# Five ring buffers for gathered rows and weights become seven of two kinds, and ten more u tiles move ahead of the last loop

## The chip, the cores and the metric

The kernel runs on one core of a Trainium2 chip. The time is device microseconds of one launch, the median of the runs of a kernel. It is one step of a streaming encoder layer (RWKV-7 mixing, sparse attention, PEER experts) for 256 prompt tokens and 8 x 16 sample tokens, in float32 throughout. Matmuls that must be exact split each operand into a rounded upper half and a remainder ("hi" and "lo", type fp32r) and add three products.

## The reference, cut to what matters

The change lies in the last part of the layer, the PEER experts. Each token picks 16 of 16,384 experts for each of 8 heads (128 experts in all), takes its dot product with their rows of `peer_u`, and adds their rows of `peer_v` with the weights that follow.

```python
def block(hb):
    ...
    e = jnp.take_along_axis(cidx, j, axis=-1)
    g = jax.nn.softmax(sc, axis=-1)
    act = jax.nn.gelu(jnp.einsum('nhkd,nd->nhk', peer_u[e], hb).astype(jnp.float32))
    return jnp.einsum('nhk,nhkd->nd', (g * act).astype(hb.dtype), peer_v[e])
...
x = x + g2 * _peer(h2, lp['w_pq'], lp['peer_keys'], lp['peer_u'], lp['peer_v'])
```

## The kernel before, in words

The first thousand microseconds (projections, RWKV, attention, mixing, choice of experts) are not touched. The rest computes the experts in two ways at once.

**The sample tokens, sparsely** (`peer_sparse`). For each of the 128 picks of a token one "row" is made: GpSimd issues an indirect DMA (line 1593) that gathers, for the 128 tokens on the 128 partitions, the u and the v row of the chosen expert side by side, 2,048 floats per partition, 1.05 MB in all. VectorE then forms the dot product with u (line 1600), ScalarE takes the gelu and the weight (1601, 1602), and VectorE adds the weighted v row to `acc` (1606). The buffer is `raw`, from `ring()`, with EB = 3 buffers: the gather of a row waits for the `acc` instruction of the row three before it. In the last loop each gather waits also for the matmuls of the v tile five before (`pace`, line 1742).

**The prompt tokens, densely.** All 16,384 experts are run for all 256 tokens in 128 tiles of 128 experts. `dense_u(j)` loads a u tile (512 KB), multiplies it with the tokens and puts the gelu into G[j]; `dense_v(j)` loads a v tile (512 KB) and accumulates G[j] times it into four PSUM banks (`bx`, `cp`, and two `dx`). G holds NW = 76 tiles of 256 floats per partition. The other 52 go to smaller tiles: 24 of them ("OFF", NB = 24) are written to DRAM from `gO` and loaded back into `gB` when needed, the others stay in 8 `gA` buffers.

The order in the program is: u tiles 0 to 41 with plain float32 matmuls; u tiles 42 to 75 with hi/lo halves; then 64 steps that make the matrix of weights and multiply G by it (`weights`), between which `ahead` adds u tiles from the list AHEAD (24 OFF and 7 more, 31 in all, at UR = 0.5 per step); then the loop over the 128 v tiles, which also makes the 21 u tiles left. Into all this `pull` weaves the rows, at a rate per step given by SR: 0.5 per u tile from tile 30 on, 0.5 per weight step, 0.62 per v tile, which makes 6, 17, 32 and 73 rows. A v tile is split into halves (lines 233 and 237, `wh` on ScalarE and `wl` on VectorE) except every third one up to the 108th, which is multiplied in plain float32.

**Buffers for tiles.** u and v tiles share a ring of four buffers `w` of 1,024 floats (`self.slots`). In the last loop the tiles of G are used up in rising order, and the kernel adds their space to the ring: after v tiles 3, 7, ... 31 four tiles of G at a time, eight buffers in all, so that the ring grows from four to twelve. A load into such a buffer shows in the trace as `G<-in_pv` or `G<-in_puT`.

**What sets the order.** A scheduler places the instructions of each engine by its own model of time, so that an engine's order isn't that of the program; on the chip each engine then runs its list strictly in order, and so does SP, which issues the direct DMAs. After the 123rd v tile come the last parts of the rows' result (`residual(0, ...)`), after the loop `finish_v` closes the four banks one by one and `residual` (lines 1576 to 1578) multiplies, adds and stores them.

Of the kernel before, what the change touches and what calls it, by code (L numbers as in the profile page):

```python
# [177 lines left out]
ORDER = "GGIggggR1R23DMMMGRMRDMRGMGMRMDGMMRRMGDMMMGGGMGGM"  # L178


N1, NW, NA, NB = 42, 76, 8, 24
SCORES, TURNS = 18, (21, 39)
SR, UR = (0.5, 0.5, 0.62), 0.5
S0, PH = 30, 4
OFF = [j for j in range(NW, 128) if (j - NW + 1) * NB // (128 - NW) > (j - NW) * NB // (128 - NW)]
AHEAD = sorted(OFF + [j for j in range(NW, 128) if j not in OFF][:NA - 1])
LAST, EARLY, SLOTS = 126, 108, 8
WB, EB = (4, 4, 3), 3
UENG, VENG, GENG, VN = 'v', 'v', 'g', 3
SENG = 'gv'  # L190
# [7 lines left out]
class K:  # L198
    def __init__(self, ctx, tc, I, O):
        self.ctx, self.tc, self.nc, self.I, self.O = ctx, tc, tc.nc, I, O  # L200
        self.uid = 0
        self.const = self.open(ctx, "const")
        self.stream = self.open(ctx, "stream")
        self.dram = self.open(ctx, "dram", space=bass.MemoryType.DRAM)
        self.nlo = 0
        self.slots = deque([None] * WB[0])
        self.lo_pattern = "v"

    def open(self, ctx, name, **kw):
# [1259 lines left out]

    def ring(self):  # L1470

        r = self.t([128, 2048], tag="raw", bufs=EB, pool=self.peer)
        return r[:, :1024], r[:, 1024:]

    def expert(self, src):

        s = self.slots.popleft()
        self.slots.append(s)
        if s is None:
            w = self.t([128, 1024], tag="w", bufs=WB[0], pool=self.stream)  # L1480
        else:
            w = self.G[:, 4 * s:4 * s + 4].rearrange("p a b -> p (a b)")
        self.nc.sync.dma_start(w, src)
        return w

# [124 lines left out]
    def run(self):  # L1610
# [79 lines left out]
        def pull(rate):  # L1690
            sn[0] += rate
            while sn[0] >= 1:
                sn[0] -= 1
                next(sparse, None)
# [46 lines left out]
        for n, j in enumerate(order):  # L1741
            self.pace = self.vdone[n - 5] if n > 4 else None
            pull(SR[2])
            while todo and sum(u not in OFF for u in gs) < NA - 1:
                u = todo.pop(0)
                gs[u] = self.dense_u(u)
            last.append(self.dense_v(j, gs.pop(j) if j >= NW else self.G[:, j], out, n))
            if j < 4 * SLOTS and j % 4 == 3:
                self.slots.append(j // 4)
            if n == 122:  # L1750
                for _ in sparse:
                    pass
                (a, b), (y, _) = self.ring(), self.ring()
                self.residual(0, [self.acc[:, c * 512:c * 512 + 512] for c in range(2)], self.gate2(0, a), self.x1_rows(0, b), y)
                (a, b), (c, y1), (y2, _) = (self.ring() for _ in range(3))
                g, x1, y = self.gate2(1, a), [self.x1_rows(1, b), self.x1_rows(2, c)], (y1, y2)
# [28 lines left out]
```

## Time and profile before

| | before |
|---|---|
| median of 3 runs | 1776.36 us (1776.22 to 1776.38) |
| the profiled execution | 1775.95 us |
| its span, first to last instruction | 1773.9 us |
| TensorE busy | 1664.8 us, 94% |
| VectorE busy | 1354.5 us, 76% |
| ScalarE busy | 750.9 us, 42% |
| GpSimd busy | 549.8 us, 31% |
| DMA | 437.22 MB, mean 246 GB/s |
| mean granted TensorE clock | 0.971 |

2.05 us of the profiled execution lie outside its span. PE is TensorE, PEld its loads of weights, DVE VectorE, ACT ScalarE, POOL GpSimd, SP the engine that issues direct DMAs. A line of the trace names the output, then the inputs; "x58" counts instructions; the bracket at its end is the idle time of the engine before it and what ended it. Neither TensorE's busy share nor a mean of one matmul tells its speed, since matmuls overlap: their starts do, 0.227 us apart for 512 columns in fp32r and about 0.118 us for 256. The page's 40 slices are 44.3 us each.

### The profile page before, as it was taken

The page shows a single profiled execution, that of the slowest core. Times are in us where ns is not written, and L with a number is a line of the kernel's source. Part 1 is how long each engine was busy: PE and PEld are TensorE (multiplying, and loading weights), DVE is VectorE, ACT ScalarE, POOL GpSimd, SP SyncE. Part 2 cuts the span into 40 slices and gives each one's busy share as a digit, 9 for nine tenths or more (in the row PEclk, how much of TensorE's full clock was granted, in tenths as well). Part 3 has the DMA queues.
Part 4 walks back from the last instruction along what each step waited for, and adds up shares of the span by engine and source line. Part 5 has one row for each costly group of instructions (what it writes and reads, how often), then busy time and mean ns, then how long its engine had stood idle before and what let it go on. Part 6 is the DMA issues. An engine that isn't in the chain of part 4 may idle for free. (4 is left out here: it accounts for less than half of the span.)

```text
span 1773.9 us, 33227 instructions
## 1 busy us (share of the span) xinstructions
PE 1664.8 (94%) x12376; PEld 1412.1 (80%) x12376; DVE 1354.5 (76%) x2905; ACT 750.9 (42%) x1666; POOL 549.8 (31%) x621
## 2 busy tenths in 40 slices
PE   6999999999999988999999989999999999999970
PEld 4898788878878866998887889999876777777750
DVE  4449788878768845566999998999766676777896
ACT  4533433333333233444222365678733343434531
POOL 2434243333332310034123223431233123223332
PEclk8999999999999999999999999999999999999995
DMA  8543752463364276655598989986499989999957
GB/s 296 164 141 99 214 173 72 157 202 110 102 220 143 79 260 209 211 177 187 188 374 322 347 326 390 381 296 203 168 377 404 357 331 360 338 343 338 333 211 258
DMA packets 173049, 437.22 MB, mean 246 GB/s; under 512 B 46036, under 2 KB 86612, under 8 KB 156504
## 3 DMA queue, kind: packets, MB, share of 16 engines
q1 hardware_dynamic: 154456, 300.89, 50.2%
q0 software_dynamic: 18432, 134.23, 20.0%
q8 instruction: 97, 1.59, 0.4%
q14 instruction: 64, 0.52, 0.1%
HBM read 403.75 MB, written 31.30 MB: 245 GB/s over the span
## 5 line engine op out<-in xcount | busy, mean ns | idle before, releaser
L1593 POOL DMA_INDIRECT raw<-in_puv,pe x128 | 177.3, 1385 | 501.9 <-DVE acc L1606 319.7
L237 DVE TENSOR_TENSOR wl<-w,wh 128x1024 fp32r<-128x1024 f32 x208 | 261.1, 1260 | 91.8 <-ACT wh L233 35.3
L233 ACT ACTIVATE wh<-w 128x1024 fp32r<-128x1024 f32 x216 | 226.9, 1053 | 152.0 <-PE mm L229 71.0
L229 PE MATMUL fx<-h2h,wh 128*128 128x256 f32 x688 | 196.5, 286 | 0.2 <-ACT G L1509 0.2
L229 PE MATMUL fx<-h2h,wl 128*128 128x256 f32 x688 | 193.9, 283 | 2.1 <-DVE wl L237 2.1
L229 PE MATMUL fx<-h2l,wh 128*128 128x256 f32 x688 | 193.6, 282 | 0.0
L1606 DVE SCALAR_TENSOR_TENSOR acc<-raw,dots,acc 128x1024 f32<-128x1024 f32 x127 | 163.5, 1287 | 21.4 <-ACT dots L1602 20.6
L1600 DVE SCALAR_TENSOR_TENSOR raw<-raw,sh 128x1024 f32<-128x1024 f32 x128 | 159.8, 1249 | 15.2 <-DMA raw<-in_puv,pe 15.1
L229 PEld LDWEIGHTS fx<-h2h,wl 128*128 128x128 f32 x688 | 130.0, 189 | 3.7 <-DVE wl L237 3.1
L229 PEld LDWEIGHTS fx<-h2h,wh 128*128 128x128 f32 x688 | 129.9, 189 | 2.5 <-issue 1.2
L229 PEld LDWEIGHTS fx<-h2l,wh 128*128 128x128 f32 x688 | 129.7, 189 | 2.2 <-issue 1.7
L229 PE MATMUL mm<-LTh,wh 128*128 128x384 f32 (+2 forms) x352 | 123.7, 352 | 1.4 <-ACT wh L233 0.8
L229 PE MATMUL mm<-LTl,wh 128*128 128x384 f32 (+2 forms) x352 | 122.1, 347 | 1.4 <-POOL LTl L490 1.4
L229 PE MATMUL mm<-LTh,wl 128*128 128x384 f32 (+2 forms) x352 | 122.5, 348 | 0.0
L237 DVE TENSOR_TENSOR wl<-G,wh 128x1024 fp32r<-128x1024 f32 x66 | 84.9, 1288 | 47.3 <-issue 29.2
L1601 ACT ACTIVATE dots<-dots 128x1 f32<-128x1 f32 x128 | 25.4, 198 | 193.5 <-DVE raw L1600 193.4
L229 PE MATMUL mm<-h2f,w 128*128 128x256 f32 x464 | 105.4, 381 | 0.0
L229 PE MATMUL mm<-wh,LTh 128*128 128x256 f32 x336 | 99.0, 295 | 1.9 <-ACT qx L893 1.9
L229 PE MATMUL mm<-wl,LTh 128*128 128x256 f32 x336 | 100.0, 298 | 0.0
L229 PE MATMUL mm<-wh,LTl 128*128 128x256 f32 x336 | 98.7, 294 | 0.0
L229 PEld LDWEIGHTS mm<-h2f,w 128*128 128x128 f32 x464 | 87.5, 190 | 12.4
L229 PE MATMUL fx<-h2f,w 128*128 128x256 f32 x336 | 78.1, 385 | 0.0
(604 smaller groups left out, 4375.4 us busy)
## 6 DMA issues: line engine op xcount, KB each, us to landing
w<-in_puT SPq DMA_DIRECT2D x118, 512.0 KB, 6.7
G<-in_pv SPq DMA_DIRECT2D x74, 512.0 KB, 5.9
w<-in_w_in SPq DMA_DIRECT2D x70, 512.0 KB, 4.5
w<-in_pv SPq DMA_DIRECT2D x54, 512.0 KB, 6.2
w<-in_w_ada SPq DMA_DIRECT2D x48, 512.0 KB, 4.7
cKT<-in_cKT SPq DMA_DIRECT2D x32, 256.0 KB, 4.1
cV<-in_cV SPq DMA_DIRECT2D x32, 256.0 KB, 4.0
w<-in_w_pq SPq DMA_DIRECT2D x16, 512.0 KB, 3.7
```

The lines of the kernel that those rows point to most:

```text
L229: return self.nc.tensor.matmul(out, l, r, start=start, stop=stop, skip_group_check=True, **kw)
L233: self.nc.scalar.activation(hi, src, AF.Copy)
L237: (self.nc.vector if eng == "v" else self.nc.gpsimd).tensor_tensor(lo, src, hi, op=OP.subtract)
L1593: d = nc.gpsimd.indirect_dma_start(out=bass.AP(tensor=u.tensor, offset=u.offset, ap=[u.ap[0], [1, 2048]]), out_offset=None, in_=self.I["puv"],
L1600: nc.vector.scalar_tensor_tensor(u, u, 1.0, h2, op0=OP.mult, op1=OP.mult, accum_out=dot)
L1601: nc.scalar.activation(dot, dot, AF.Gelu_apprx_tanh)
L1606: nc.vector.scalar_tensor_tensor(acc, v, dot, acc, op0=OP.mult, op1=OP.add)
```

## The change

Three things change in the last part.

- G's space is given out in another way as it is used up. The string `RWRWRWW` says in which order: R is a buffer for a row (eight tiles of G), W one for a tile (four tiles). So the ring of `raw` grows from three to six (at v tiles 7, 19 and 31) and the ring of `w` from four to eight (at v tiles 11, 23, 35 and 39) in place of twelve.
- NB goes from 24 to 34: ten more tiles are OFF, written to DRAM and loaded back. AHEAD has 41 tiles in place of 31, at a rate of 0.65 per weight step in place of 0.5; the last loop makes 11 u tiles in place of 21.
- Rows are pulled at 0.58 per weight step (37 rows in place of 32) and 0.58 per v tile (68 in place of 73). The last one is pulled at v tile 117, as before.

```diff
-N1, NW, NA, NB = 42, 76, 8, 24
+N1, NW, NA, NB = 42, 76, 8, 34
 SCORES, TURNS = 18, (21, 39)
-SR, UR = (0.5, 0.5, 0.62), 0.5
+SR, UR = (0.5, 0.58, 0.58), 0.65
...
-LAST, EARLY, SLOTS = 126, 108, 8
+LAST, EARLY = 126, 108
+FREED = {}
+for _k in "RWRWRWW":
+    _a = max((j + 1 for j in FREED), default=0)
+    FREED[_a + (7 if _k == "R" else 3)] = (_k, _a)
...
     def ring(self):
-        r = self.t([128, 2048], tag="raw", bufs=EB, pool=self.peer)
+        s = self.rslots.popleft()
+        self.rslots.append(s)
+        if s is None:
+            r = self.t([128, 2048], tag="raw", bufs=EB, pool=self.peer)
+        else:
+            r = self.G[:, s:s + 8].rearrange("p a b -> p (a b)")
         return r[:, :1024], r[:, 1024:]
...
-            w = self.G[:, 4 * s:4 * s + 4].rearrange("p a b -> p (a b)")
+            w = self.G[:, s:s + 4].rearrange("p a b -> p (a b)")
...
-            if j < 4 * SLOTS and j % 4 == 3:
-                self.slots.append(j // 4)
+            if j in FREED:
+                kind, a = FREED[j]
+                (self.slots if kind == "W" else self.rslots).append(a)
```

The computation and the number of instructions for it are the same, but for ten more stores and ten more loads of 128 KB. Up to the middle of the u tiles with halves every engine's list is the same. Line numbers of the changed kernel are higher: 1600 becomes 1610, 1606 becomes 1616, 1576 becomes 1586 and 237 becomes 242.

**VectorE, the end of its list.** `wl` is the lower half of a v tile and `Gl` that of its G, on which TensorE waits; `raw,dots` and `acc` are the two instructions of a row. Before, around the last two `wl`:

```order
L1600 SCALAR_TENSOR_TENSOR raw_17979,dots_17981<-raw_17979,sh_2289_11699 128x1024
L237 TENSOR_TENSOR wl_18744<-G_11076,wh_18743 128x1024
L237 TENSOR_TENSOR Gl_18749<-gA_18023,Gh_18748 128x256
L1606 SCALAR_TENSOR_TENSOR acc_11701<-raw_17950,dots_17952,acc_11701 128x1024
L237 TENSOR_TENSOR wl_18754<-G_11076,wh_18753 128x1024
L237 TENSOR_TENSOR Gl_18761<-gB_18757,Gh_18760 128x256
L1606 SCALAR_TENSOR_TENSOR acc_11701<-raw_17979,dots_17981,acc_11701 128x1024
L1600 SCALAR_TENSOR_TENSOR raw_18046,dots_18048<-raw_18046,sh_2289_11699 128x1024
L1606 SCALAR_TENSOR_TENSOR acc_11701<-raw_18046,dots_18048,acc_11701 128x1024
L1600 SCALAR_TENSOR_TENSOR raw_18074,dots_18076<-raw_18074,sh_2289_11699 128x1024
```

And in the changed kernel, from the last row on:

```order
L1610 SCALAR_TENSOR_TENSOR G_11076,dots_18544<-G_11076,sh_2289_11699 128x1024
L1616 SCALAR_TENSOR_TENSOR acc_11701<-G_11076,dots_18544,acc_11701 128x1024
L1586 TENSOR_TENSOR raw_18684<-acc_11701,raw_18683 128x512 x2
L242 TENSOR_TENSOR wl_18709<-G_11076,wh_18708 128x1024
L242 TENSOR_TENSOR Gl_18646<-gB_18642,Gh_18645 128x256
L242 TENSOR_TENSOR Gl_18668<-G_11076,Gh_18667 128x256
L242 TENSOR_TENSOR Gl_18718<-gB_18712,Gh_18717 128x256
L242 TENSOR_TENSOR wl_18735<-G_11076,wh_18734 128x1024
L242 TENSOR_TENSOR Gl_18739<-G_11076,Gh_18738 128x256
L242 TENSOR_TENSOR wl_18756<-G_11076,wh_18755 128x1024
```

Before, 115 rows have their dot product ahead of the last `wl`, and 13 rows stand behind it; in the changed kernel all 128 rows and the residual of the sample tokens stand ahead of the last five `wl`.

**VectorE, in the middle of the last loop.** A row before:

```order
L1606 SCALAR_TENSOR_TENSOR acc_11701<-raw_16180,dots_16182,acc_11701 128x1024
L237 TENSOR_TENSOR wl_16510<-G_11076,wh_16509 128x1024
L237 TENSOR_TENSOR wl_16555<-w_16551,wh_16554 128x1024
L237 TENSOR_TENSOR Gl_16591<-G_11076,Gh_16590 128x256
L1600 SCALAR_TENSOR_TENSOR raw_16246,dots_16248<-raw_16246,sh_2289_11699 128x1024
L1606 SCALAR_TENSOR_TENSOR acc_11701<-raw_16246,dots_16248,acc_11701 128x1024
```

and two rows in the changed kernel, the first of them in space of G:

```order
L1610 SCALAR_TENSOR_TENSOR G_11076,dots_16398<-G_11076,sh_2289_11699 128x1024
L242 TENSOR_TENSOR Gl_16477<-gA_13835,Gh_16476 128x256
L1616 SCALAR_TENSOR_TENSOR acc_11701<-G_11076,dots_16398,acc_11701 128x1024
L1610 SCALAR_TENSOR_TENSOR raw_16424,dots_16426<-raw_16424,sh_2289_11699 128x1024
L242 TENSOR_TENSOR Gl_16544<-G_11076,Gh_16543 128x256
L1616 SCALAR_TENSOR_TENSOR acc_11701<-raw_16424,dots_16426,acc_11701 128x1024
```

Counted over the whole loop by the numbers in the names: before, a row's dot product stands mostly four to six v tiles behind the `acc` that frees its buffer, and falls behind the tile that paces it, from 7 tiles at the start of the loop to 36 at its end. In the changed kernel it stands 9 to 12 tiles behind the `acc` that frees the buffer as a rule (4 at the least), and 5 to 11 behind the tile that paces it, all along the loop.

**TensorE, the start of the last loop.** `mm`, `bx` and `cp` from `oh` are the weight steps, `fx` the u tiles (24 matmuls each), `bx<-w,G` the first v tiles. Before:

```order
L229 MATMUL mm_15167<-oh_15164 128x128 x4
L229 MATMUL bx_15181<-oh_15174 128x128 x4
L229 MATMUL mm_15234<-oh_15231 128x128 x4
L229 MATMUL bx_15269<-w_15278,G_11076 128x512
L229 MATMUL bx_15269<-w_15291,G_11076 128x512
L229 MATMUL bx_15269<-w_15297,G_11076 128x512
L229 MATMUL cp_15248<-oh_15241 128x128 x4
L229 MATMUL fx_15393<-h2h_11870,wh_15394 128x256
```

and in the changed kernel, where the last weight step lies 17 rows further up:

```order
L234 MATMUL fx_15601<-h2h_11870,wh_15602 128x256
L234 MATMUL fx_15601<-h2l_11871,wh_15602 128x256
L234 MATMUL fx_15601<-h2h_11870,wl_15603 128x256
L234 MATMUL bx_15644<-w_15653,G_11076 128x512
L234 MATMUL bx_15644<-w_15666,G_11076 128x512
L234 MATMUL bx_15644<-w_15672,G_11076 128x512
L234 MATMUL cp_15645<-w_15653,G_11076 128x512
```

Of the 86 u tiles with halves (42 to 127), 65 stand ahead of the first v tile before and 75 now. About five of the ten more stand between weight steps 32 and 40, three or four between step 56 and the end.

More of the change, by code (lines that the diff above doesn't have):

```diff
@@ L206, in __init__ @@
         self.slots = deque([None] * WB[0])
+        self.rslots = deque([None] * EB)
         self.lo_pattern = "v"
```

## The prediction

> **What bounds the kernel now.** The first view is the page's row of 40 slices: busy tenths of TensorE and VectorE, and the share of the 16 DMA engines.
>
> ```profile
> PE   6999999999999988999999989999999999999970
> DVE  4449788878768845566999998999766676777896
> DMA  8543752463364276655598989986499989999957
> ```
>
> TensorE is full up to slice 38 and stops there; VectorE and the DMA engines go on. The second view cuts the part that changes into stages (columns: length, busy time and count of PE, PEld, DVE, ACT and POOL, clock, DMA share, GB/s).
>
> ```profile
> 1040.00:1120.00 80.00, 79.21 (x682) 78.50 (x681) 71.35 (x80) 43.13 (x89) 27.15 (x16) 1.00 0.96 372
> 1160.00:1280.00 120.00, 117.91 (x1000) 115.43 (x999) 114.12 (x164) 99.21 (x261) 31.89 (x29) 1.00 0.65 225
> 1280.00:1718.00 438.00, 436.00 (x1905) 321.82 (x1903) 318.62 (x376) 179.77 (x342) 135.75 (x114) 1.00 0.91 338
> 1290.00:1380.00 90.00, 88.57 (x403) 66.23 (x402) 63.99 (x76) 35.16 (x68) 32.98 (x31) 1.00 1.03 400
> 1360.00:1680.00 320.00, 320.00 (x1405) 235.34 (x1404) 230.39 (x272) 131.45 (x246) 92.12 (x77) 1.00 0.94 348
> 1718.00:1761.00 43.00, 4.07 (x6) 1.17 (x4) 29.86 (x37) 7.05 (x26) 14.54 (x10) 0.56 0.77 278
> ```
>
> The first is the u tiles with halves, the second most of the weight stage, the third the whole last loop, with two pieces of it, the last the time behind it. Up to 1718 us TensorE sets the pace: in the loop it is busy 436.00 of 438 us. The weight stage has 35% of the DMA engines free, the loop 9%. Behind 1718 us TensorE does nothing that matters, which the timeline of the end shows (start, length, what; in the bracket the wait before it):
>
> ```profile
> 1717.90 0.39 PE L229 MATMUL dx<-wh,Gl 128*128 128x512 f32 x1
> ...
> 1733.20 1.23 DVE L1600 SCALAR_TENSOR_TENSOR raw<-raw,sh 128x1024 f32<-128x1024 f32 x1 [1.75 <-DMA raw<-in_puv,pe]
> ...
> 1758.27 2.68 DVE L1606 SCALAR_TENSOR_TENSOR acc<-raw,dots,acc 128x1024 f32<-128x1024 f32 x2
> ...
> 1764.65 0.69 DVE L1576 TENSOR_TENSOR raw<-bx,raw 128x512 f32<-128x512 f32 x1 [2.37 <-POOL raw L1577]
> ...
> 1769.13 1.29 DVE L1577 TENSOR_TENSOR raw<-raw,raw 128x512 f32<-128x512 f32 x2 [0.77 <-DMA raw<-d]
> ```
>
> The last matmul ends at 1718.3. Then rows are still being made until 1761.0, one in some 3.6 us, VectorE waiting for their gathers; the residuals follow until 1770.4 and their stores until 1773.9. So the end is 55.6 us that only the rows' lateness causes. How many rows fall where is in the `acc` instructions of line 1606 by stage:
>
> ```profile
> 0.00:1160.00 1160.00, 65.77 (x51) 0.98 0.63 213
> 1160.00:1280.00 120.00, 7.65 (x6) 1.00 0.65 225
> 1280.00:1718.00 438.00, 74.67 (x58) 1.00 0.91 338
> 1718.00:1774.00 56.00, 15.41 (x12) 0.56 0.74 261
> ```
>
> 58 rows in the loop are one in 7.6 us, though the program pulls 0.62 per v tile, one in 5.5 us. What holds them back is in the waits inside the loop and in the landing times of its gathers:
>
> ```profile
> POOL raw L1593 <- DVE acc L1606: 204.2, 40, 9.7
> ...
> L1593 POOL DMA_INDIRECT raw<-in_puv,pe x61: 936/1184/1890, 1293.1 to 1718.0; - x61
> ...
> DMA to landing us min/median/max: 5.5/8.2/10.5
> ```
>
> GpSimd stands 204 of 438 us before a gather because none of the three buffers is free: `acc` of the row three before hasn't run. It hasn't run because VectorE's list puts it there, not because VectorE is late; VectorE is busy 319 of 438 us.
>
> **The change, part by part.**
>
> *The rows.* With six buffers the new list has all 128 rows ahead of the last five `wl`, so the 12 rows behind 1718.3 move into the time that TensorE fills. Where do they fit? Five more are made ahead of the loop (63 in place of 58 by VectorE's list) and 65 in it. A row costs VectorE 1.27 + 0.08 + 1.29 = 2.64 us and a u tile's lower half 1.30 us:
>
> ```profile
> L1606 DVE SCALAR_TENSOR_TENSOR acc<-raw,dots,acc 128x1024 f32<-128x1024 f32 x58 | 74.7, 1287 | 14.9 <-ACT dots L1602 14.5
> L1600 DVE SCALAR_TENSOR_TENSOR raw<-raw,sh 128x1024 f32<-128x1024 f32 x58 | 73.9, 1274 | 0.5 <-DMA raw<-in_puv,pe 0.5
> L237 DVE TENSOR_TENSOR wl<-w,wh 128x1024 fp32r<-128x1024 f32 x44 | 57.4, 1304 | 30.8 <-PE dx L229 10.7 <-ACT wh L233 10.2 <-issue 6.9
> ...
> L1600 DVE DVE_READ_ACCUMULATOR raw<-raw,sh 128x1 f32 x58 | 4.7, 81 | 0.0
> ```
>
> In the loop VectorE then has 318.6 + 7 x 2.64 - 10 x 1.30 = 324 us to do in about 410 (below): covered, 79%.
>
> *Ten u tiles go from the loop to the weight stage.* Each is 24 matmuls in a row of 2.83 us in the chain of waits; the loop's last gate matmuls are in the timeline:
>
> ```profile
> 1414.90 2.83 PE fx L229 x24
> ...
> 1702.76 1.88 PE L229 MATMUL fx<-modr,clate 128*128 128x512 f32 x4
> ```
>
> 28.3 us of TensorE leave the loop (438 becomes 409.7) and enter the stage: nothing in sum, if TensorE sets the pace in both. In 1160 to 1280 VectorE has 114.1 us, and gains 10 x 1.30 + 5 x 2.64 = 26.2, in all 140.3; TensorE has 117.9 and gains 28.3, in all 146.2. So TensorE stays the longer one, by 6 us; I put 1 us for a stall there. The stage still has four buffers `w`. That such a ring feeds TensorE at one u tile in 2.83 us shows in 1040 to 1120: 79.21 of 80 us busy at 372 GB/s. If that cover were gone, ten tiles would wait for their loads at about 6.5 us each less 2.83, some 37 us; I take none of it, since there the same thing ran.
>
> *Ten more stores and loads of 128 KB.* The loop's DMAs before:
>
> ```profile
> DMA packets 46246, 148.11 MB, mean 338 GB/s; under 512 B 3838, under 2 KB 20222, under 8 KB 38655
> ...
> w<-in_pv SPq DMA_DIRECT2D x48, 512.0 KB, 6.5
> ...
> w<-in_puT SPq DMA_DIRECT2D x10, 512.0 KB, 6.8
> G<-in_puT SPq DMA_DIRECT2D x10, 512.0 KB, 4.9
> gB<-d SPq DMA_DIRECT2D x24, 128.0 KB, 5.6
> raw<-in_puv,pe POOLq DMA_INDIRECT x61, 8.2
> ```
>
> The loop loses ten u loads (5.2 MB), gains ten `gB` (1.3 MB) and one to four gathers of 1.05 MB: 145 to 149 MB, I take 148. But it has 409.7 us in place of 438: **361 GB/s** in place of 338. This is the price of the change, and the trace shows the rate reached: 400 GB/s over the 90 us from 1290 to 1380, while TensorE was busy 88.57 of 90. Its own waits from 1290 to 1718 add up to this:
>
> ```profile
> PE bx L229 <- ACT wh L233: 1.0, 1, 1.0
> PE bx L229 <- DVE wl L237: 0.4, 1, 0.4
> ```
>
> So 1.43 us lost in 90 us of full DMA. A loop that is full all along loses 1.43 x 410 / 90 = 6.5 us, of which 2 are in it now: 5 us more, with the stage's 1 us **6 us**. The bounds: 0, if nothing of it shows, and 28.3, if the loop can move no more than its 338 GB/s and so takes 438 us as before.
>
> The Trainium skill has a rule against this step: "DMA: Bandwidth & Descriptors", "Where 436 GB/s comes from", gives about 358 GB/s as what HBM has for one core, binding between HBM and SBUF. By it the loop would need 148 / 0.358 = 413 us, 3.7 more than TensorE, and the sum below would lie at 1731 before any other stall. The trace doesn't agree, with 400 GB/s over 90 us.
>
> *The ring of `w` ends at eight in place of twelve,* and gets its first extra buffer at v tile 11, not 3. The split that empties a buffer and half the matmuls of a tile that isn't split (two of its four banks) are here:
>
> ```profile
> L233 ACT ACTIVATE wh<-w 128x1024 fp32r<-128x1024 f32 x216 | 226.9, 1053 | 152.0 <-PE mm L229 71.0
> ...
> 1401.53 1.72 PE dx L229 x4
> ```
>
> Eight buffers at 3.2 us per v tile (409.7 / 128) give a load over 20 us; it lands in 6.5. Until tile 11, the 17th in the loop's order, there are four: 12.8 us for a load of 6.5, a split of 1.05 + 1.30, and 3.4 more for a tile that isn't split. That is close, and a rival below. Taken at nothing.
>
> *The end.* Two gate matmuls that ran behind the loop now run in it: 1.9 us. Behind the last matmul are left one multiply and one add (1.29 / 2 each), 0.2 for signals, and the stores, 1773.9 - 1770.4 = 3.5: 5.0 us. The other banks close 6 x 0.227 = 1.4 us apart, time for their 1.3 us of VectorE. The residual of the sample tokens is hidden under the last five v tiles.
>
> **The sum:** 1718.3 + 1.9 + 6 + 5.0 = 1731.2 us of span; with the 2.05 us outside it (1775.95 - 1773.9) 1733.2; the median lies 0.4 above that execution: **1733.6 us**. Without a stall it would be 1727.6.
>
> **The rivals.**
>
> 1. *The DMA engines become the bound of the loop.* For it: from 1360 to 1680 they are 94% busy at 348 GB/s, which at 100% is 370, near the 361 wanted and near the 372 of tiles up to 117, where the rows end. Against it: the 400 GB/s, and that more gathers in flight keep the engines fuller. At 348 GB/s the loop takes 148 / 0.348 = 425 us, 15.6 more: 1743. At 338, 28.3 more: 1756.
> 2. *The ring of four runs dry at the start of the loop and in the weight stage.* Loads then land in 10 us in place of 6.5; a tile takes (10 + 2.4 + 3.4) / 4 = 3.95 us against 3.2, over 16 tiles 12 us: 1740. Against it: 1290 to 1380, where the ring grew from five to eight, lost 1.43 us.
> 3. *Slower: late gathers hold up VectorE, and the tiles stand behind them.* A row is now ahead of a `wl` in VectorE's strict order, so a late row stops TensorE once its three split tiles (about 9 us) are used up. By the list a row has 5 to 11 v tiles, 16 to 35 us, from its pace to its use; a gather needs 1.2 us of GpSimd and 8.2 to land. It decides once landing takes over 16 us, twice the median. Then each of the 65 rows must cost 0.75 us for the 48.7 us to be gone; at 0.85 us each the time is 1727.6 + 55 = 1783. Against it: the longest landing was 10.5 us, at 400 GB/s too.
> 4. *The rows are late all the same and the end stays.* The lists are fixed and have no row behind the last `wl`, so this would have to be rival 3. At most no difference, 1776.
>
> **How the numbers follow.** Chances: the forecast 0.66 (1726 to 1740), rival 1 0.20 (1740 to 1757), rival 2 0.08 (1738 to 1746), rival 3 0.04, rival 4 0.02. The range that leaves out at most 2 in 10 is the forecast with nearly all of rival 1, from 1725 (no stall, and 2 us better at the end) to 1757. A change of 0.2% (3.6 us) can be told from none: faster 0.94, same 0.02, slower 0.04.
>
> **What would show it.** Right: no row's `acc` behind the last matmul; the chain of waits ending in PE, then one `dx` multiply, an add and a store; the last matmul at 1720 to 1730 us; some 360 GB/s in a loop of 410 to 420 us; ten more `gO` stores. Wrong: GpSimd still waiting some 200 us for `acc`; VectorE waiting on gathers inside the loop; TensorE waiting for `wl` at each row (rival 3) or for loads (rivals 1 and 2); a weight stage longer by more than 30 us.

## The result: 0.7% faster, 30 us short of the forecast

| | before | changed |
|---|---|---|
| median (six runs each) | 1776.37 us (1772.91 to 1777.25) | 1763.61 us (1756.88 to 1769.11) |
| ratio | 1 | 0.9928, 95% interval 0.9904 to 0.9952 |
| the profiled execution, its span | 1775.95, 1773.9 us | 1769.11, 1767.3 us |
| first matmul of a v tile | 1278.1 us | 1312.3 us |
| from there to the end of the last matmul | 440.2 us | 450.4 us |
| behind the last matmul | 55.6 us | 4.6 us |

Forecast were 1733.6 us and a range from 1725 to 1757. The kernel is faster, but by 12.8 us in place of 42.8. The profiled execution of the changed kernel is the slowest of its six, 5.5 us over their median; the accounts below are of that execution.

The page's slices of the changed kernel show TensorE full to the end, and the DMA engines at nine tenths or more in eight of the last ten slices, which are the loop:

```profile
PE   6999999999999988999999999999999999999987
...
DMA  8543652464365276655498999998669999899992
```

The rows of the windows (columns as in the prediction) for the weight stage, the loop, and its middle part:

```profile
1160.00:1310.00 150.00, 146.53 (x1269) 145.25 (x1268) 141.32 (x194) 114.83 (x295) 42.75 (x34) 1.00 0.74 258
1310.00:1762.00 452.00, 425.40 (x1684) 300.94 (x1683) 329.33 (x396) 168.01 (x343) 140.91 (x120) 0.97 0.90 341
1340.00:1700.00 360.00, 343.44 (x1338) 238.07 (x1339) 271.46 (x324) 132.71 (x277) 116.57 (x98) 0.98 0.97 369
```

In the loop TensorE is busy 425.4 of 452 us; before it was 436 of 438. The end is as forecast. In its timeline there is no `acc` behind the last matmul, only a multiply, an add and a store:

```profile
1762.36 0.39 PE L234 MATMUL dx<-wh,Gl 128*128 128x512 f32 x1
1762.78 0.69 DVE L1586 TENSOR_TENSOR G<-dx,G 128x512 f32<-128x512 f32 x1
...
1763.51 0.69 DVE L1587 TENSOR_TENSOR G<-G,raw 128x512 f32<-128x512 f32 x1
```

So the 51 us at the end were won, and most of that was given back in the loop: by the prediction it was to be 440.2 - 28.3 (ten u tiles fewer) + 1.9 + 5 = 418.8 us, and it is 450.4. TensorE's own waits in it are these (columns: us in total, times, longest):

```profile
PE bx L234 <- ACT Gh L238: 15.2, 4, 8.3
PE bx L234 <- ACT wh L238: 4.6, 4, 1.9
PE bx L234 <- DVE wl L242: 2.4, 4, 0.9
PE fx L234 <- DVE wl L242: 1.5, 2, 0.8
PE bx L234 <- DVE Gl L242: 1.5, 1, 1.5
PE bx L234 <- DMA w<-in_pv: 1.3, 1, 1.3
```

26.5 us in all, where before had 1.4; only 1.3 of them end directly with a load. More than half is for `Gh`, the upper half of a tile of G. ScalarE makes it, but it waits for somebody else; the other engines' waits in the same time say for whom:

```profile
POOL raw L1603 <- PE dx L234: 115.8, 28, 6.5
POOL G L1603 <- PE dx L234: 92.6, 24, 6.9
...
ACT Gh L238 <- POOL gB L1538: 30.1, 10, 6.0
...
POOL raw L1587 <- DVE raw L1586: 22.2, 1, 22.2
```

GpSimd hardly waits for `acc` any more before a gather (18.1 us in four places; 204.2 before). It waits for the pace, 208.4 us in 52 places, and GpSimd's list is strict too: what stands behind a waiting gather waits with it. That is the multiply of `gB` or `gA` by its weights (line 1538), from which `Gh` is made. The worst place is the last row, the add of the sample tokens' residual (line 1587). GpSimd's and then TensorE's timeline there:

```profile
1736.08 3.85 POOL L1587 TENSOR_TENSOR raw<-raw,raw 128x512 f32<-128x512 f32 x2 [22.21 <-DVE raw L1586]
1739.89 1.41 POOL L1538 TENSOR_TENSOR gB<-gB,Ws 128x256 f32<-128x256 f32 x2
...
1741.11 0.80 PE L234 MATMUL bx<-wh,Gh 128*128 128x512 f32 x1 [8.25 <-ACT Gh L238]
1741.70 0.63 PE L234 MATMUL cp<-wh,Gh 128*128 128x512 f32 x1
1742.13 0.63 PE L234 MATMUL bx<-wl,Gh 128*128 128x512 f32 x1
```

GpSimd stands 22.21 us because the add waits for VectorE's multiply behind the last row's `acc`. Four `gB` multiplies come after it, two at once and two later; TensorE, which needs them, stands 8.25 us. Its matmuls then start 0.43 us apart in place of 0.227, since the granted clock is 0.50. A gap of 1.94 us at 1510 had the same sequel, and there are five such stretches in the loop (the matmul behind that gap, then the windows of the five, clock in the third column from the right):

```profile
1510.36 0.70 PE L234 MATMUL bx<-wh,Gh 128*128 128x512 f32 x1 [1.94 <-ACT wh L238]
...
1510.40:1513.80 3.40, 3.40 (x8) 2.67 (x9) 2.31 (x3) 0.18 (x1) 0.00 (x0) 0.51 1.02 398
1524.20:1527.50 3.30, 3.30 (x9) 2.52 (x9) 2.08 (x3) 1.93 (x4) 2.60 (x3) 0.50 0.94 369
1647.10:1650.40 3.30, 3.30 (x9) 2.53 (x9) 2.79 (x6) 1.89 (x5) 0.09 (x1) 0.50 0.92 338
1688.00:1691.30 3.30, 3.30 (x10) 2.51 (x9) 3.30 (x5) 0.90 (x4) 0.12 (x1) 0.50 1.04 421
1735.80:1745.70 9.90, 4.59 (x11) 3.62 (x12) 4.92 (x7) 1.57 (x5) 6.67 (x6) 0.50 0.23 79
```

At half the clock half of TensorE's busy time is lost: (3.40 + 3 x 3.30 + 4.59) / 2 = 9 us, an estimate from these rows. With the 26.5 us of waits that is 35.5 of the 36.6 us that the loop is longer than 440.2 - 28.3 + 1.9 = 413.8. The Trainium skill, "TensorE: Matmul & The Clock Gate", "Part 1: The HAM clock gate", says that the array gets half its clock pulses after at least one idle window of about 3.4 us; the trace agrees for the gap of 8.25 us, and shows the same behind one of 1.94.

### The profile page after: what moved, and what is told of

It reads as the page before. It is cut to its first block, busy times and chain, and to the rows that moved or that the text cites. A ratio compares the mean times of both kernels' runs of the same rounds, so it can differ in the third digit from the quotient of the medians.

```text
span 1767.3 us, 33186 instructions
## 1 busy us (share of the span) xinstructions
PE 1678.8 (95%) x12376; PEld 1416.6 (80%) x12376; DVE 1353.2 (77%) x2905; ACT 744.1 (42%) x1666; POOL 545.4 (31%) x621
## 4 chain that ended last, share of the span: by engine, by line
PE 56%; DVE 20%; DMA 9%; issue 8%; POOL 4%; ACT 3%; SPq 1%; POOLq 0%; DVEq 0%; ACTq 0%
PE mm L234 21%; PE dx L234 11%; PE fx L234 8%; PE cp L234 7%; PE bx L234 6%; DVE acc L1616 3%; DVE wl L242 3%; DVE raw L1610 2%; DMA raw<-in_puv,pe 2%; DMA w<-in_puT 2%; ACT wh L238 1%; DMA w<-in_w_ada 1%; POOL raw L1603 1%; DVE TX L708 1%; DMA w<-in_pv 1%
## 5 line engine op out<-in xcount | busy, mean ns | idle before, releaser
L242 DVE TENSOR_TENSOR wl<-w,wh 128x1024 fp32r<-128x1024 f32 x238 | 299.5, 1263 | 96.2 <-ACT wh L238 57.2
L238 ACT ACTIVATE wh<-w 128x1024 fp32r<-128x1024 f32 x246 | 257.9, 1052 | 161.6 <-PE mm L234 70.5
L1603 POOL DMA_INDIRECT raw<-in_puv,pe x101 | 139.7, 1383 | 351.4 <-DVE acc L1616 132.7
L1616 DVE SCALAR_TENSOR_TENSOR acc<-raw,dots,acc 128x1024 f32<-128x1024 f32 x100 | 132.3, 1323 | 13.9 <-ACT dots L1612 13.8
L1610 DVE SCALAR_TENSOR_TENSOR raw<-raw,sh 128x1024 f32<-128x1024 f32 x101 | 125.5, 1243 | 10.2 <-DMA raw<-in_puv,pe 10.1
L234 PEld LDWEIGHTS fx<-h2f,w 128*128 128x128 f32 x336 | 65.3, 196 | 10.1 <-issue 0.7
```

The lines of the kernel that those rows point to most:

```text
L234: return self.nc.tensor.matmul(out, l, r, start=start, stop=stop, skip_group_check=True, **kw)
L238: self.nc.scalar.activation(hi, src, AF.Copy)
L242: (self.nc.vector if eng == "v" else self.nc.gpsimd).tensor_tensor(lo, src, hi, op=OP.subtract)
L1603: d = nc.gpsimd.indirect_dma_start(out=bass.AP(tensor=u.tensor, offset=u.offset, ap=[u.ap[0], [1, 2048]]), out_offset=None, in_=self.I["puv"],
L1610: nc.vector.scalar_tensor_tensor(u, u, 1.0, h2, op0=OP.mult, op1=OP.mult, accum_out=dot)
L1616: nc.vector.scalar_tensor_tensor(acc, v, dot, acc, op0=OP.mult, op1=OP.add)
```

## The experiments

Three theories stand against each other. **A**: the order on GpSimd, as just read. **B**: rival 1 of the prediction, the DMA engines are the loop's bound. **C**: VectorE's list, in which halves stand behind rows. A fourth, **D**, the ring of `w` is too short, comes in with experiments 6 and 7. All experiments start from the changed kernel; they are told by subject, with the numbers in which they were made. "Loop" is from the first matmul of a v tile to the end of the last, as in the table above; it is of one profiled execution, the medians are of four runs or more. An edit can make the scheduler plan other engines' lists anew; where that matters, the text says how many instructions of the loop keep their order, by the names in the two traces.

### The order on GpSimd

**Experiment 1: the multiplies on VectorE.**

```diff
-UENG, VENG, GENG, VN = 'v', 'v', 'g', 3
+UENG, VENG, GENG, VN = 'v', 'v', 'v', 3
```

> The changed kernel (median 1763.6 us), but the 52 multiplies of gA and gB by their weights run on VectorE, so that none stands behind a gather or behind the residual's add in GpSimd's strict list. Theory A (order on GpSimd: a gather waits for the pace, or the residual's add for the last acc, and the next gB multiply stands behind it; TensorE then waits and its clock drops after the longer gaps): the waits of TensorE for Gh, 15.2 us, fall under 3 us, the clock goes back to 1.00 but for the end, 1735 to 1748 us. Theory B (the loop is bound by the DMA engines, 364 to 378 GB/s at a share of 0.96 to 1.00, and the gaps are late loads under another name): the gaps stay with other names, 1757 to 1769 us. Against both: VectorE gets some 52 instructions more, and if these delay wl it is 1765 us or more.

Measured: 1748.46 us, ratio to before 0.9841 (0.9824 to 0.9857); loop 433.0 us. 15 us better than the changed kernel, half a microsecond over what A expected at most. The waits for `Gh` go from 15.2 to 4.3 us. The other lists stay nearly as they were: 320 of ScalarE's 339 instructions in the loop keep their order.

**Experiment 2: only the residual's add on VectorE.**

```diff
-            (nc.vector if i else nc.gpsimd).tensor_tensor(y[:, cols], y[:, cols], x1[:, cols], op=OP.add)
+            nc.vector.tensor_tensor(y[:, cols], y[:, cols], x1[:, cols], op=OP.add)
```

> The changed kernel, but the two adds of the sample tokens' residual run on VectorE, behind the multiply that they wait for anyway; GpSimd's list is else the same. Theory A1 (the 22.2 us wait of this add on GpSimd holds the last four gB multiplies, TensorE stands 8.25 us and then runs at half clock for some 8 us, another 4 us): 1750 to 1755 us, no gap over 2 us behind 1730 us, the other Gh waits (7 us) as they are. Theory B (DMA): no difference, 1757 to 1769 us.

Measured: 1757.53 us, ratio 0.9883 (0.9867 to 0.99); loop 444.7 us. 6 us, where 9 to 14 were expected: the gap is halved, not gone. Its next cause shows in the timelines of ScalarE and TensorE:

```profile
1731.08 0.20 ACT L1611 ACTIVATE dots<-dots 128x1 f32<-128x1 f32 x1 [3.32 <-DVE G L1610]
...
1731.52 1.99 ACT L238 ACTIVATE wh<-G 128x1024 fp32r<-128x1024 f32 x2
1733.41 0.40 ACT L238 ACTIVATE Gh<-gB 128x256 fp32r<-128x256 f32 x1
...
1733.87 0.50 PE L234 MATMUL bx<-wh,Gh 128*128 128x512 f32 x1 [4.15 <-ACT Gh L238]
```

ScalarE waits for the last row's dot product, to take its gelu, and two `wh` and the `Gh` stand behind that. It is the same fault on another engine.

**Experiment 8: four buffers `gB` in place of two.** This leaves each engine its work and each byte its way; it only lets the multiplies stand further up in GpSimd's list.

```diff
-            g = self.t([128, 256], tag="gB", bufs=2)
+            g = self.t([128, 256], tag="gB", bufs=4)
```

> The changed kernel (1763.6 us) with four buffers gB in place of two, nothing else: each engine does the same work, all multiplies stay on GpSimd and the DMA engines move the same bytes. By GpSimd's list a gB tile now lies 8 to 19 v tiles ahead of the pace of the gather before it (1 to 9 in the changed kernel from the 20th tile on), and no multiply is left behind the residual's add. Theory A (order on GpSimd): the waits for Gh go from 15.2 us to under 3 us, the clock's dips behind them too, 1742 to 1750 us. Theory B (full DMA engines): 1757 to 1769 us.

Measured: 1751.50 us, ratio 0.9872 (0.984 to 0.9904); loop 435.1 us. TensorE's waits:

```profile
PE bx L234 <- ACT wh L238: 10.4, 8, 2.0
PE bx L234 <- DVE wl L242: 2.4, 4, 0.9
PE fx L234 <- DVE wl L242: 0.8, 1, 0.8
PE fx L234 <- ACT wh L238: 0.6, 1, 0.6
```

No wait for `Gh` is left, and the time falls by 12 us, to 1.5 over A's range and 5.5 under B's. A is shown, by two edits (this and experiment 1) that have nothing else in common. But the waits for `wh` go from 4.6 to 11.0 us: another cause appears as the first is taken away. Experiment 10 shows which.

### The parts of the change alone

**Experiment 3: the rings alone,** with 24 OFF tiles and the old rates.

```diff
-N1, NW, NA, NB = 42, 76, 8, 34
+N1, NW, NA, NB = 42, 76, 8, 24
-SR, UR = (0.5, 0.58, 0.58), 0.65
+SR, UR = (0.5, 0.5, 0.62), 0.5
```

> The first part of the change alone: the new rings of rows and weights, with 24 OFF tiles and the rates of before (0.5, 0.5, 0.62 and 0.5). The loop is then some 438 us long again, with all rows in it: about 161 MB, 367 GB/s, as dense as in the changed kernel. By the lists a gB multiply's tile lies 4 to 15 v tiles ahead of the pace of the gather before it (1 to 9 in the changed kernel), and the residual's add has only one gB multiply behind it. Theory A (order on GpSimd): TensorE waits under 5 us for Gh, 1730 to 1745 us. Theory B (DMA engines): the same stalls as in the changed kernel, 1757 to 1769 us.

Measured: 1751.68 us (1741.5 to 1757.74), ratio 0.9853 (0.9808 to 0.9898); between A's forecast and B's. The trace has no wait for `Gh`, as A says, and 8.1 us for `wh`, of which more at experiment 10; the loop is 461.3 us, of which 28.3 are the ten u tiles, so 433.0 like the others.

**Experiment 4: the rest alone:** 34 OFF tiles and the new rates, with the rings of before.

```diff
-for _k in "RWRWRWW":
+for _k in "WWWWWWWW":
```

> The other parts of the change alone: 34 OFF tiles and the new rates, but three buffers of rows all along and eight more of weights as before. By the lists 12 rows stand behind the last wl again. Every theory: GpSimd waits about 200 us for acc, the last matmul ends at 1720 to 1725 us, about 50 us of rows behind it, 1768 to 1778 us. Theory A: TensorE waits under 3 us for Gh in the loop, since the gathers lag far behind their pace. Theory that the ten moved tiles themselves cost the time: the loop is 430 us or longer and the time 1780 us or more.

Measured: 1778.45 us, ratio 1.0014 (1.0001 to 1.0027). Its loop is 417.8 us, near the 418.8 that the prediction had for the changed kernel, at 338 GB/s; the rows lie behind it, as before. Moving ten u tiles costs nearly nothing by itself (2 us) and brings nothing by itself. The gain, and most of the stall, come with the rows.

### The DMA engines

**Experiment 5: half of each row is gathered,** on top of experiment 1 (`GENG = 'v'`).

```diff
-                d = nc.gpsimd.indirect_dma_start(out=bass.AP(tensor=u.tensor, offset=u.offset, ap=[u.ap[0], [1, 2048]]), out_offset=None,
-                                                 in_=self.I["puv"],
+                d = nc.gpsimd.indirect_dma_start(out=bass.AP(tensor=u.tensor, offset=u.offset, ap=[u.ap[0], [1, 1024]]), out_offset=None,
+                                                 in_=bass.AP(tensor=self.I["puv"].tensor, offset=self.I["puv"].offset, ap=[[1024, 32768], [1, 1024]]),
...
-                    nc.vector.scalar_tensor_tensor(acc, v, dot, acc, op0=OP.mult, op1=OP.add)
+                    nc.vector.scalar_tensor_tensor(acc, u, dot, acc, op0=OP.mult, op1=OP.add)
```

> As the first experiment (multiplies on VectorE, 1748.5 us), but each gather reads only 1,024 of the 2,048 floats of a row (the v half is left out and the product with u is added in its place, so the sums are other numbers); the number of instructions is the same on every engine. The loop then moves about 34 MB less, some 114 MB or 275 GB/s. Theory B (what is left over the forecast after the order on GpSimd is mended, 15 us, comes from full DMA engines: 383 GB/s at a share of 1.00, loads of tiles land late): 1728 to 1737 us, no wait of TensorE over 1 us for wh or w. Theory C (what is left is VectorE's list, in which multiplies and halves stand behind rows): 1744 to 1751 us, the waits of 3.16 us (Gh) and 2.23 us (wl) as they are.

Measured: 1811.27 us, ratio 1.0182 (1.0163 to 1.02), which no theory expected. The scheduler planned the stage before anew for the shorter gathers; there TensorE now waits 66.8 us for VectorE's choice of experts (`pix`). The total therefore says nothing on the loop. The loop itself is 430.7 us, only 2.3 less than in experiment 1, though the DMA engines have a fifth of their time free in it:

```profile
1376.70:1807.50 430.80, 418.27 (x1666) 295.03 (x1664) 329.26 (x449) 165.36 (x339) 83.45 (x68) 0.99 0.80 279
```

TensorE waits 12.4 us in it for VectorE and ScalarE. That speaks against B as the only cause of what is left.

**Experiment 9: the same, but in the last loop alone.** The pace is set only there, so the size (and, in lines not shown, the view of `puv` and the choice of u for v) hangs on it.

```diff
+ap=[u.ap[0], [1, 2048 if self.pace is None else 1024]]
```

> As the first experiment (multiplies on VectorE, 1748.5 us), but the gathers of the last loop alone read 1,024 floats of a row in place of 2,048 (there the product with u is added in place of v, so the sums are other numbers). The part ahead of the loop is as in the first experiment, unlike the fifth. The loop moves some 30 MB less, about 300 GB/s. Theory B (what is left over the forecast, 15 us, comes from full DMA engines): 1730 to 1738 us. Theory C (VectorE's list: halves and multiplies stand behind rows): 1743 to 1751 us, waits of TensorE of 8 us or more between 1310 and 1740 us.

Measured: 1739.60 us, ratio 0.9796 (0.9769 to 0.9823); loop 425.1 us. 9 us less than experiment 1: most of what B expected, 1.6 us over its range. Waits of 9.4 us for VectorE and ScalarE are left, so C has a share. The lists of TensorE, VectorE, ScalarE and GpSimd in the loop are those of experiment 5, instruction for instruction, and with the same bytes its loop was 430.7: so far apart are two single executions. They are not those of experiment 1: 233 of ScalarE's 339 instructions keep their order, and 291 of VectorE's 450.

**Experiment 10: multiplies and the residual's add on VectorE, and four `gB`:** the edits of experiments 1, 2 and 8 together.

> As the first experiment (multiplies on VectorE), with the residual's add on VectorE too and four buffers gB, so that VectorE's list can have the multiplies earlier. Theory C (VectorE's list): the waits for Gh of 1.10 and 3.16 us near 1700 and 1717 us and the half clock behind them go, 1740 to 1746 us. Theory B: 1746 to 1751 us.

Measured: 1747.53 us, ratio 0.9847 (0.9821 to 0.9874); loop 434.3 us. The `Gh` waits are gone, but against experiment 1 `wh` is waited for 7.8 us in place of 3.3, and nearly nothing is won. Experiments 1, 3, 8 and 10, four kernels with four different lists, stop at 1747.5 to 1751.7 us, with loops of 433.0 to 435.1 us (28.3 taken off in experiment 3). That could be a common floor; what the waits for `wh` are says otherwise. The first of the seven, on ScalarE and on TensorE:

```profile
1368.73 0.42 ACT L238 ACTIVATE Gh<-gB 128x256 fp32r<-128x256 f32 x1 [4.80 <-PE dx L234]
1369.06 0.19 ACT L1611 ACTIVATE dots<-dots 128x1 f32<-128x1 f32 x1
1369.15 1.04 ACT L238 ACTIVATE wh<-w 128x1024 fp32r<-128x1024 f32 x1
...
1370.24 0.50 PE L234 MATMUL bx<-wh,Gh 128*128 128x512 f32 x1 [1.09 <-ACT wh L238]
```

ScalarE stands 4.80 us with a `Gh` that waits for TensorE, and the `wh` that TensorE needs next stands behind it in the list. The load of its tile had landed 2.4 us earlier, by the trace's semaphores. All seven are like this: `wh` starts right behind another instruction of ScalarE, and in six its load had landed 2.4 to 15 us earlier, in one (1.0 of the 7.8 us) 0.3 us. So these are hardly late loads but again the order of a list, now ScalarE's.

**Experiment 11: experiment 10 with the half rows of experiment 9.**

> As the tenth experiment (multiplies and the residual's add on VectorE, four gB, 1747.5 us), with the half gathers in the loop of the ninth (30 MB less; the product with u is added in place of v, so the sums are other numbers). Theory B with A (order on GpSimd and full DMA engines are the two causes, and little else): the waits for wh and the loads behind them (7.8 us) go, 1732 to 1739 us, near the forecast 1733.6. Theory C (VectorE's list costs as much on its own): 1743 us or more.

Measured: 1736.13 us, ratio 0.9778 (0.9762 to 0.9794); loop 418.2 us, again the 418.8 of the prediction. What TensorE still waits for:

```profile
PE bx L234 <- DVE wl L242: 4.4, 6, 1.4
PE fx L234 <- DVE wl L242: 0.8, 1, 0.8
```

These 5.2 us are C's share. The waits for `wh` are gone, as B says. But the scheduler planned these lists anew too (232 of ScalarE's 339 instructions in the loop keep their order, 291 of VectorE's 452), and ScalarE's own waits show it (experiment 10's row, then those of this one):

```profile
ACT Gh L238 <- PE dx L234: 160.3, 75, 4.8
...
ACT wh L238 <- DMA G<-in_pv: 29.4, 10, 5.2
ACT wh L238 <- DMA w<-in_pv: 28.9, 17, 4.3
ACT wh L238 <- DMA w<-in_puT: 17.2, 5, 5.9
ACT Gh L238 <- PE dx L234: 10.4, 9, 1.6
```

ScalarE now runs ahead of TensorE until a load stops it; TensorE doesn't notice. So fewer bytes and another order came together, and the run doesn't tell which of them brought the 16.1 us of the loop.

**Experiments 12 and 13: 13.1 MB more.** Experiment 10 with 100 DMAs of 128 KB from DRAM to DRAM whose output nobody reads; in the second with a wait that ties each to its place in the loop. The lines are those of the second, without the line that makes `more`; the first has no wait and the v tiles 8 to 107.

```diff
+        if 10 <= n < 110:
+            d = self.nc.sync.dma_start(self.more[n - 10], self.I["pv"][j * 128:(j + 1) * 128, :256])
+            self.tc.add_manual_dep(d.ins, self.vdone[n - 9], mybir.DependencyInfo(
+                mybir.DependencyClass.Sync, mybir.DependencyReason.DATA), reason="more")
```

> As the tenth experiment (1747.5 us), with 100 more DMAs of 128 KB in the loop, from DRAM to DRAM, one ahead of the load of gB of v tiles 8 to 107 (13.1 MB more; nothing waits for them and nothing of the result changes). Theory B (full DMA engines set the loop's floor): 13.1 MB at 0.38 GB/ms are 34 us of their time, of which some is absorbed at the loop's end, where they are idle: 1762 to 1782 us, with waits for wh of 20 us and more. Theory C: 1746 to 1752 us.

Measured: 1783.37 us, ratio 1.0032 (1.0018 to 1.0046), near what B expected and yet no evidence for it. The first matmul of a v tile is at 1348.5 us in place of 1306.2, and the loop 433.2 us, no longer than without. Nothing held the new DMAs, and all 100 were issued by 110 us; TensorE was busy 59.8 of the first 100 us, 83.9 in experiment 10. The experiment missed the loop, so it was done again:

> As the twelfth experiment, whose 100 extra DMAs all ran at the program's start, but each now waits for the matmuls of the v tile nine before its own, which are long done when its turn comes in SP's list, so that they lie between the loads of v tiles 10 to 109 (13.1 MB more in the loop; the tenth experiment's loop took 434 us). Theory B (full DMA engines set the loop's floor): 13.1 MB at 0.38 GB/ms are 34 us of their time, some of it absorbed at the loop's end: the time is 1762 to 1782 us, the loop 448 to 468 us, with 20 us and more of waits for wh, wl and w. Theory C (VectorE's list): 1746 to 1752 us.

Measured: 1766.60 us, ratio 0.9947 (0.9929 to 0.9965); loop 449.7 us. 19 us more in the time, 15 in the loop. Time, loop and waits lie in B's ranges, and over 360 us the engines moved more than in experiment 10 (its rows first, then one of experiment 13, TensorE's waits there, and one of SP's):

```profile
1340.00:1700.00 360.00, 351.53 (x1391) 244.20 (x1390) 281.29 (x378) 137.66 (x289) 76.34 (x62) 1.00 0.99 378
...
1720.00:1745.00 25.00, 18.85 (x82) 14.94 (x80) 18.17 (x27) 7.98 (x12) 0.00 (x0) 1.00 0.17 64
...
1340.00:1700.00 360.00, 341.02 (x1332) 232.25 (x1331) 268.04 (x360) 130.53 (x271) 71.69 (x60) 1.00 1.02 397
...
PE bx L234 <- ACT wh L238: 17.0, 14, 2.9
PE bx L234 <- DVE wl L242: 5.6, 8, 2.5
...
SPq L1529 <- PE dx L234: 38.5, 30, 3.4
```

Yet this is no clean test either. Of the 15 waits for `wh` (18.0 us, one of them with `fx`) three, 2.6 us, begin with a load that has just landed; in the others `wh` stands behind something else on ScalarE, whose list was planned anew (267 of 339 keep their order). And SP's list is strict too: SP stands 88.8 us before the extra DMAs (line 1529), 38.5 of them for the very matmuls that were to be long done, and the loads of tiles stand behind them.

So 34.1 MB less (65 gathers by 0.52 MB) went with a loop 2 to 16 us shorter, 13.1 MB more with one 15 us longer, and each time the lists changed with the bytes. That full DMA engines cost something is likely; that they set a floor at 433 us is not shown, and the traces of experiments 5 and 10 speak for the order of the lists. What would settle it is experiment 10 with half gathers and its lists held fixed. That was not run.

**Experiment 7: rings alone, with the new row rates:** five rows fewer in the loop, five more in the weight stage.

```diff
-SR, UR = (0.5, 0.5, 0.62), 0.5
+SR, UR = (0.5, 0.58, 0.58), 0.5
```

> As the third experiment (rings alone, 1751.7 us), but with the row rates of the changed kernel, 0.58 and 0.58: five more rows are made in the weight stage, where the DMA engines have a third of their time free, and five fewer, 5.2 MB, in the loop, where they have none. Theory B (full DMA engines in the loop): 5.2 MB at 0.385 GB/ms less there, up to 13 us, 1738 to 1745 us. Theory C or D (VectorE's list, or the ring of w): the weight stage is VectorE's, which gains 13 us of work there, and the loop's stalls stay, 1750 to 1760 us.

Measured: 1755.30 us, ratio 0.9877 (0.9858 to 0.9895), which is not faster than experiment 3. The loop is 453.0 us, 8.3 shorter, which B expects; but five rows fewer are also 13 us less work for VectorE, so it doesn't part B from C. And it begins 14.6 us later, since the weight stage became VectorE's:

```profile
1160.00:1296.00 136.00, 122.03 (x1007) 118.04 (x1006) 128.36 (x179) 102.17 (x274) 42.33 (x34) 0.99 0.67 237
```

VectorE's 128.4 us now exceed TensorE's 122.0 (in experiment 3's stage, up to 1282, they are 116.5 and 119.8), and neither fills the 136.

**Experiment 6: the ring of `w` grows first, and to eleven,** on top of experiment 1.

```diff
-for _k in "RWRWRWW":
+for _k in "WRWRWRWWWW":
```

> As the first experiment, but with the string WRWRWRWWWW: the ring of w grows first (at v tile 3 in place of 11) and to eleven buffers in place of eight; the ring of rows grows to six as before, four tiles later. Theory D (rival 2 of the prediction, and its like in the whole loop: the ring of w is too short, a load starts too late): the waits for wh and w, 4 to 5 us, and the clock's dips behind them go, 1738 to 1743 us. Theory B (full DMA engines): more buffers move nothing faster, 1746 to 1751 us.

Measured: 1758.55 us, ratio 0.9885 (0.9855 to 0.9915); loop 443.3 us. With three more buffers it is 10 us slower than experiment 1, so D's gain didn't come. But it is no clean test of D: the waits for `wh` fall a little, from 3.3 to 2.3 us, and those for `Gh` rise from 4.3 to 13.6, which is nearly the whole difference of the loops; at the longest, VectorE's list has the `gB` multiply behind the `acc` of one row, which waits 0.96 us for ScalarE, and the dot product of the next. Why the scheduler put it there wasn't followed up.

## Why the prediction was wrong, point by point

**What bounds the kernel, and the rows: right.** All 128 rows lie ahead of the last matmul, the end behind it is 4.6 us (5.0 forecast), and the chain there is as described. VectorE has 329.3 us to do in the loop, 324 forecast, and waited 2.2 us for gathers in it: rival 3's late gathers did not come, and rival 4 neither.

**Ten u tiles into the weight stage: right in kind.** The loop begins 34.2 us later, 28.3 for the tiles, 1 us of stall forecast, 5.9 found in that execution; in the experiments with the same stage (1, 2, 4, 6, 8 to 11 and 13) it begins at 1306.2 to 1311.5, which is 0 to 5 over the tiles' 28.3.

**The stalls of the loop, 5 us: wrong, and this is the step that failed.** It was 450.4 - 440.2 + 28.3 - 1.9 = 36.6 us in the profiled execution, outside even the bound of 28.3. The prediction took the 5 us from how full the DMA engines were, 1.43 us lost in 90, and put the waits of one engine's list for another at nothing. The runs showed 26.5 us of waits, all but 1.3 of them for another engine and 15.2 for a `Gh` that GpSimd held up, and 9 us of half clock behind them.

*GpSimd's list was not looked at.* The prediction saw that a gather now waits for the pace, and checked by VectorE's list that this makes no row late. It did not ask what stands behind a gather on GpSimd itself. Before, the gathers lagged 9 to 37 v tiles behind the pace and waited for `acc`, so a `gB` multiply that stood behind one was early anyway. By the changed kernel's list its tile is 1 to 9 v tiles ahead of that pace from the 50th v tile on, and the add of the residual, costed as hidden under the last five tiles, stands ahead of four of them. Price, by medians: 12.1 us by experiment 8, 15.2 by 1, 16.1 by 10.

*What is left, 13.9 us from experiment 10 to the forecast, has no cause that a run shows by itself.* The loop there stalls for 434.3 - 413.8 = 20.5 us, 14.3 of them in waits: 7.8 for `wh`, nearly all by the order on ScalarE (above), and 6.5 for `wl`, the longest, 2.6 us, behind two multiplies that had waited 3.66 us on VectorE for the load of their weights (`Ws`). The prediction looked at VectorE's list for the rows alone, and at ScalarE's not at all.

*The price of the DMA engines stays open.* The loop moved 153.9 MB, not 148: the gathers took 6.2 MB more than before, where one to four of 1.05 MB were reckoned, and the residual's loads and stores, 2.6 MB, moved in from behind the loop. And they were averaged over the whole loop, though its end needs few: in experiment 10 the engines did 378 GB/s over 360 us and 64 over the last 25. From experiment 10 to 11 the time falls by 11.4 us, but with other lists.

**Rival 1**, at 0.20, is neither shown nor ruled out: experiment 11 fits it, and experiment 5 has a loop of 430.7 us at 279 GB/s. Its rate of 348 GB/s was too low; the engines did 369 and 378 in the rows above. The section "Where 436 GB/s comes from" of "DMA: Bandwidth & Descriptors" in the Trainium skill gives about 358 GB/s for one core; the loops here kept up 369 to 397 over 360 us, so the figure is exceeded. **Rival 2** (ring of four) expected late loads at the loop's start; TensorE's one wait there that ends with a load of `w` took 1.2 us in experiment 3 and 1.3 in the changed kernel, and more buffers (6) brought no gain.

**What would show it:** the signs named as wrong had GpSimd waiting some 200 us for `acc`, and TensorE waiting for `wl` at each row or for loads. GpSimd did wait 208 us, for something else, and no sign named `Gh`.

The best kernel found is experiment 10, 1747.5 us, 16 us better than the changed one by three lines; experiment 1 is within a microsecond of it with one.

## What to carry to other kernels

When a change moves a wait from one releaser to another, go through the list of the engine that waits, and of each engine in the strict order behind it, and name what stands behind the waiting instruction; a wait that costs nothing on an idle engine costs all of it to the small helper work queued there. After a repair look at which wait has grown, and follow it one engine further back before naming it: `wh` comes from a DMA, but ScalarE's list was what held it. And where a scheduler makes the lists, an experiment that changes bytes may change the order with them; compare the lists before giving the difference to the bytes.

## What the runs showed of the hardware

- In the changed kernel TensorE ran at a granted clock of 0.51 for 3.4 us behind a gap of 1.94 us, at 0.50 for 3.3 us behind two of 1.00 and 0.55 us less than 2 us apart, and at 0.50 for 9.9 us in and behind one of 8.25 us. Not each such gap did it: in experiment 8 one of 2.01 us, at 1357, lies in a stretch of 50 us at 1.00.
- One core moved 397 GB/s over 360 us at a share of 1.02 (experiment 13), 378 at 0.99 in experiment 10.
- One multiply of 128 x 256 took 0.41 to 0.50 us on VectorE (experiment 1), and 0.72 to 1.80 on GpSimd (the changed kernel), 52 of them in either loop:

```profile
1698.70 0.42 DVE L1538 TENSOR_TENSOR gA<-gA,Ws 128x256 f32<-128x256 f32 x1
...
1710.39 1.80 POOL L1538 TENSOR_TENSOR gA<-gA,Ws 128x256 f32<-128x256 f32 x1
```
